# Row pairs in linear attention, and half-array products in longer blocks: one change to a two-layer hybrid trunk

## The chip, the cores and the metric

The kernel runs on one core of one Trainium2 chip. The metric is the device time of one execution in microseconds. Times are given for the kernel as a whole; the profile is one further execution, recorded by the hardware profiler.

## The reference: what is computed

The model is a trunk of two layers over 256 latent tokens and 256 context tokens of width 1024, all in fp32. In each layer one input projection feeds three token mixers and their gates. The mixers are latent attention with 8 heads (MLA), bidirectional gated linear attention with 4 heads (GLA) and neighbourhood attention with 8 heads. Their outputs are merged by gates, and a SwiGLU block follows. The change touches the two softmax mixers a little and the linear attention a lot. What the linear attention computes, cut to its core:

```python
q, k, v, log_a = ch(q), ch(k), ch(v), ch(log_a)      # chunks of 64 tokens
cum = jnp.cumsum(log_a, axis=3)
q_dec = q * jnp.exp(cum)
k_inv = k * jnp.exp(-cum)
k_end = k * jnp.exp(last - cum)
att = jnp.where(lower, einsum('bhncd,bhnsd->bhncs', q_dec, k_inv), 0.0)
o_intra = einsum('bhncs,bhnse->bhnce', att, v)
kv_chunk = einsum('bhncd,bhnce->bhnde', k_end, v)
# scan over chunks: state = decay * state + kv_chunk
o_inter = einsum('bhncd,bhnde->bhnce', q_dec, s_prev)
```

It is done forward and backward in time; context tokens come first and hand their final state to the latent tokens. In the last layer context tokens give no output, so only the two latent token tiles need attention there.

In the softmax mixers the latent queries see 512 keys (latent and context), the context queries 256 (context only); the latter are left out in the last layer.

## The kernel before, in words

Activations lie with features on the 128 partitions and the 512 tokens along the free dimension. The weight matrices are streamed from HBM in units of 128 x 1024 (`take`), each split by ScalarE (`hi`) and VectorE (`lo`) into two fp32r parts, and each product of the projections is three matmuls (`gemm`). The small products of the mixers are plain fp32; the profiler records each such product as two TensorE instructions.

The program isn't issued in the order in which it is written. `_Plan` records every operation with a price (`price`) and its dependencies, gives each a due time (TensorE's operations in the order recorded, the others backwards from who needs them), and `schedule` plays the engines against each other with those prices: each engine takes the ready operation with the earliest due time whose buffers have a free slot. There are 8 PSUM banks (`b`) and 70 SBUF slabs of 128 x 512 (`s`). The order that comes out is emitted as it is, and each engine then runs its own list in that order, waiting on semaphores. `drive` interleaves the recording: it runs the main work, a list of projections, and draws a filler generator along, so that the sum of the filler's yielded costs keeps pace with the mains' share done (`ftotal` is the sum at which the mains end). Lines 253 to 260 change the price of one kind of matmul: where the output has 64 partitions or fewer and the one before it went to another set of partitions, the second costs 56 ns (27 for 32 partitions).

The stages that matter here, in each layer:

- `fill1` (MLA) and `fill2` (neighbourhood attention) run `softmax_items` as filler: per head pair `hp`, key set `s` (0: latent queries, 1: context queries), query half `q` and head `e`, a score bank (`mas`, `nas`), the softmax, transposes into `PT` slabs (`mat`, `nat`), and `st_O`, which multiplies by the values. The two heads of a pair write to partitions 0-63 and 64-127 of one bank (`mao`, `nao`), so their products use different column halves of the array.
- `gla` is the filler of the next stage, whose mains are the values and gates of the linear attention (`zt`) and the merge of branch 1 (`z`, `proj`). `gla_prep` makes the cumulated decays: per head `hh` one bank `gc`, for each of four token tiles `t` a product with the upper triangle into partitions 0-63 and one with the lower into 64-127 (forward and backward). `ec` and `ei` are their exponentials, by which `qq` and `kk` are scaled.
- `kv(t)` transposes the scaled keys of one token tile (`gkt`, copied to `gkT`), and for each of its two chunks of 64 tokens multiplies keys by values: `gkv`, with 64 rows of the array (the chunk's tokens, partitions 0-63 or 64-127) and 128 columns, four heads into one bank. VectorE scales each head's block by the chunk's decay (`gkvs`).
- `att(t)` makes, for each direction `d`, the products of keys and queries of the four heads into one bank `gat`; the direction's 64 features are partitions 0-63 or 64-127, so again 64 rows and 128 columns. VectorE copies them under a mask (`attz`), and adds the two (`gatt`).
- `scan` carries the states (`gS`, on VectorE), and `o_tile` forms the output (`go`): values by `gatt`, queries by the states. Token tiles 2 and 3 (context) come first, then 0 and 1. After `gla`, its output `yB` is merged by branch 2, the last before the output projection (`wo`).

Of the kernel before, what the change touches and what calls it, by code (L numbers as in the profile page):

```python
# [9 lines left out]
F32 = mybir.dt.float32  # L10
# [171 lines left out]
class _Plan:  # L182
# [15 lines left out]
    def record(self, eng, name, args, kw):  # L198
        op = _Op()
        op.eng, op.name, op.args, op.kw, op.idx = eng, name, args, kw, len(self.ops)  # L200
        op.func = args[2] if name == "activation" else None
        w, r = [], []
        if "out" in kw:
            w.append(kw["out"])
            rest = list(args)
        else:
            w.append(args[0])
            rest = list(args[1:])
        for k, v in kw.items():
            if k == "accum_out":  # L210
                w.append(v)
            elif k != "out":
                rest.append(v)
        r = [v for v in rest if isinstance(v, _View)]
        w = [v for v in w if isinstance(v, _View)]
        if name == "copy_predicated" or (name == "matmul" and not kw.get("start", True)):
            r.append(w[0])
        deps = set()
        op.bufs = []
        op.allocs = []  # L220
        for v in r:
            g = v.region()
            deps.update(o for o, q in v.buf.writes if _meets(g, q))
        for v in w:
            g = v.region()
            if v.buf.space == "psum" and eng == "pe":
                prev = [o for o, q in v.buf.writes]
                deps.update(prev[-1:])
                deps.update(o for o, q in v.buf.reads)
            else:  # L230
                deps.update(o for o, q in v.buf.writes if _meets(g, q))
                deps.update(o for o, q in v.buf.reads if _meets(g, q))
        for v in r:
            v.buf.reads.append((op.idx, v.region()))
        for v in w:
            g = v.region()
            if v.buf.first is None:
                v.buf.first = op.idx
                op.allocs.append(v.buf)
            v.buf.writes = [x for x in v.buf.writes if not (g[4] is None and x[1][0] >= g[0] and x[1][1] <= g[1] and x[1][2] >= g[2] and x[1][3] <= g[3])]  # L240
            v.buf.reads = [x for x in v.buf.reads if not (g[4] is None and x[0] != op.idx and x[1][0] >= g[0] and x[1][1] <= g[1] and x[1][2] >= g[2] and x[1][3] <= g[3])]
            v.buf.writes.append((op.idx, g))
        for b in {id(v.buf): v.buf for v in r + w}.values():
            op.bufs.append(b)
            b.left += 1
        deps.discard(op.idx)
        op.deps = deps
        op.pin = self.last_pe if self.pinned else None
        op.cost, op.bytes = self.price(eng, name, w, r, kw)
        if eng == "pe":  # L250
            self.last_pe = op.idx
            rows = w[0].p1 - w[0].p0
            if name == "matmul" and r[0].dtype == F32 and rows <= 64:
                if self.lead and w[0].p0 not in self.lead:
                    op.cost = 56.0 if rows > 32 else 27.0
                    self.lead.add(w[0].p0)
                else:
                    self.lead = {w[0].p0}
            else:
                self.lead = set()  # L260
        self.ops.append(op)
        return op
# [227 lines left out]
def tile_trunk(ctx: ExitStack, tc: tile.TileContext, xin, wst, wm0, wmt, cbc_in, ct_in, cols_in, fin_in,  # L490
# [18 lines left out]
    if True:  # L509
# [215 lines left out]
        def softmax_items(lat_only, S_fn, V, heads, bias_fn, fin_fn, name):  # L725

            items = [(hp, s, q, e) for hp in range(heads // 2) for s in range(1 if lat_only else 2) for q in range(2) for e in range(2)]
            P, PT, PO = {}, {}, {}

            def st_S(it):  # L730
                hp, s, q, e = it
# [26 lines left out]
                    nc.scalar.copy(PT[hp, s, e][a][:, :, 128 * q : 128 * q + 128], ps[:, 2 * a : 2 * a + 2])  # L758
                return 107 * n

            def st_O(hp, s):
                n = 4 if s == 0 else 2
                if s == 0:
                    PO[hp] = bank(f"{name}o{hp}")
                pt = [PT.pop((hp, s, e)) for e in range(2)]
                for k in range(n):
                    for e in range(2):
                        c = 128 * hp + 64 * e
                        nc.tensor.matmul(PO[hp][64 * e : 64 * e + 64, 256 * s : 256 * s + 256], V[2 * s + k][:, c : c + 64], pt[e][k // 2][:, k % 2],
                                         start=(k == 0), stop=(k == n - 1))  # L770
                if s == 1 or lat_only:
                    w = 256 if lat_only else 512
                    fin_fn(hp, PO.pop(hp)[:, :w], w)
                return 429 * n

            n = len(items)
            pend = []
            for i in range(n + 4):
                if i < n:
                    yield st_S(items[i])  # L780
                if 2 <= i < n + 2:
                    it = items[i - 2]
                    yield st_T(it)
                    if it[2] == 1 and it[3] == 1:
                        pend.append((i + 1, it[0], it[1]))
                if pend and pend[0][0] <= i:
                    _, hp, s = pend.pop(0)
                    yield st_O(hp, s)
            for _, hp, s in pend:
                yield st_O(hp, s)  # L790


        NF = 5
# [134 lines left out]
        for l in range(L):  # L928
# [275 lines left out]

            def gla_prep(las):
                for hh in range(4):
                    ps = bank("gc", [128, 512])
                    for t in range(4):
                        for d in range(2):
                            nc.tensor.matmul(ps[64 * d : 64 * d + 64, 128 * t : 128 * t + 128],  # L1210
                                             las[t][:, 128 * hh + 64 * d : 128 * hh + 64 * d + 64], tri[d], start=True, stop=True)
                    ec, ei = slab("gec"), slab("gei")
                    nc.scalar.activation(ec, ps, AF.Exp, bias=zero)
                    nc.scalar.activation(ei, ps, AF.Exp, bias=zero, scale=-1.0)
                    ecv = ec.rearrange("p (c s) -> p c s", s=64)
                    nc.vector.tensor_copy(dec[0:64, hh], ecv[0:64, :, 63])
                    nc.vector.tensor_copy(dec[64:128, hh], ecv[64:128, :, 0])
                    nc.vector.tensor_tensor(out=kk[hh], in0=kk[hh], in1=ei, op=ALU.mult)
                    nc.vector.tensor_tensor(out=qq[hh][:, :NQ], in0=qq[hh][:, :NQ], in1=ec[:, :NQ], op=ALU.mult)
                    yield 1800  # L1220
# [80 lines left out]
            def gla():  # L1301
# [14 lines left out]
                    bufs.append(t)  # L1316
                ctx_out = not last

                def kv(t):
                    ps = bank("gkt", [128, 4, 128])  # L1320
                    for hh in range(4):
                        nc.tensor.transpose(ps[:, hh], kk[hh][:, 128 * t : 128 * t + 128], ident)
                    kt = slab("gkT")
                    nc.scalar.copy(kt, ps)
                    yield 430
                    for half in range(2):
                        r = slice(64 * half, 64 * half + 64)
                        c = 2 * t + half
                        pk = bank("gkv", [128, 4, 128])
                        for hh in range(4):  # L1330
                            nc.tensor.matmul(pk[:, hh], kt[r, 128 * hh : 128 * hh + 128], gv[t][r, 128 * hh : 128 * hh + 128], start=True, stop=True)
                        s = slab("gkvs", shape=[128, 4, 128])
                        for hh in range(4):
                            nc.vector.tensor_scalar(out=s[:, hh], in0=pk[:, hh], scalar1=dec[:, hh, c : c + 1], scalar2=None, op0=ALU.mult)
                        kvs[c] = s
                        yield 860

                def att(t):
                    w = slice(128 * t, 128 * t + 128)
                    a = slab("gatt")  # L1340
                    for d in range(2):
                        r = slice(64 * d, 64 * d + 64)
                        ps = bank("gat", [128, 4, 128])
                        for hh in range(4):
                            nc.tensor.matmul(ps[:, hh], kk[hh][r, w], qq[hh][r, w], start=True, stop=True)
                        nc.vector.copy_predicated(bufs[d], gmask[d], ps.rearrange("p a b -> p (a b)"))
                        yield 860
                    nc.vector.tensor_tensor(out=a, in0=bufs[0], in1=bufs[1], op=ALU.add)
                    atts[t] = a

                Sp = {}
                ys = {}
# [42 lines left out]
                for cf in ([4, 5, 6, 7], [0, 1, 2, 3]):  # L1395
                    tt = (cf[0] // 2, cf[0] // 2 + 1)
                    for t in tt:
                        yield from kv(t)
                        if t in ts:
                            yield from att(t)  # L1400
                    st = scan(cf, cf[::-1], Sp, st)
                    for t in tt:
                        if t in ts:
# [308 lines left out]
```

## Time and profile before

| | |
|---|---|
| median of 3 runs | 1548.5 us (1545.71, 1548.5, 1548.73) |
| profiled execution | 1543.93 us, span 1542.1 us |
| mean granted TensorE clock | 0.996 |
| TensorE busy | 1523.3 us (99%), 9566 matmul instructions |
| weight loads | 1311.6 us (85%) |
| VectorE (DVE) busy | 1089.3 us (71%), 2174 instructions |
| ScalarE (ACT) busy | 763.3 us (49%), 1363 instructions |
| `gkv`: 128 instructions, 372.8 to 1254.7 us | `gat`: 96, 379.6 to 1261.6 us |
| `gc`: 128 instructions, 345.9 to 1212.5 us | `mao`, `nao`: 160 each |

Layer 0 of the linear attention lies at about 334 to 482 us of the span, layer 1 at about 1184 to 1290. The duration that a row gives for one matmul is longer than the time it takes from the next one, since matmuls overlap in the pipeline; the chain of waits, which adds up without overlap, gives what a group really takes. Some matmul records can be missing from a trace.

### The profile page before, as it was taken

The numbers are of one execution on the slowest core, as the hardware profiler recorded it, in microseconds if no ns is written. First come the engines' busy times: TensorE is split into PE (matmuls) and PEld (weight loads), VectorE is DVE, ScalarE is ACT, GpSimd is POOL, SyncE is SP. The second block draws the span as 40 slices with busy tenths as digits, with TensorE's granted clock in tenths as the row PEclk, the third lists the DMA queues.
The fourth block names the chain that finished last, engine by engine and source line by source line (L and its number), as shares of the span: only waits on it lengthen the run. The fifth ranks groups of instructions, "written<-read, shape, count | busy, mean of one in ns | idle before, by whom it ended". The sixth has DMA issues, their size and how long they took to land.

```text
span 1542.1 us, 24547 instructions
## 1 busy us (share of the span) xinstructions
PE 1523.3 (99%) x9566; PEld 1311.6 (85%) x9566; DVE 1089.3 (71%) x2174; ACT 763.3 (49%) x1363; POOL 0.2 (0%) x4
## 2 busy tenths in 40 slices
PE   8999999999999999999999999999999999999998
PEld 4687787789877899888888889887998999999998
DVE  5799989989888789633333336898476797776565
ACT  4669745576223345332232234679567535564443
POOL 0000000000000000000000000000000000000000
PEclk9999999999999999999999999999999999999999
DMA  9442244533335775622223224432342234455553
GB/s 365 148 157 99 101 157 168 172 131 123 103 110 174 248 268 179 204 93 91 92 90 100 96 91 143 143 113 82 105 145 87 99 107 164 164 195 190 178 190 112
DMA packets 67157, 222.68 MB, mean 144 GB/s; under 512 B 7964, under 2 KB 8348, under 8 KB 67040
## 3 DMA queue, kind: packets, MB, share of 16 engines
q1 hardware_dynamic: 67040, 221.11, 42.1%
q8 instruction: 75, 1.23, 0.3%
q14 instruction: 42, 0.34, 0.1%
HBM read 220.03 MB, written 1.05 MB: 143 GB/s over the span
## 4 chain that ended last, share of the span: by engine, by line
PE 94%; ACT 3%; DVE 2%; issue 0%; DMA 0%; SPq 0%; DVEq 0%
PE z L486 22%; PE fg L486 12%; PE fu L486 12%; PE fo L486 12%; PE zt L486 8%; PE proj L486 7%; PE wo L486 4%; PE zf L486 2%; PE mas L486 1%; PE nao L486 1%; PE nas L486 1%; PE mat L486 1%; PE go L486 1%; PE nat L486 1%; PE mao L486 1%; PE gkv L486 1%
## 5 line engine op out<-in xcount | busy, mean ns | idle before, releaser
L486 ACT CAST hi<-raw 128x1024 fp32r<-128x1024 f32 (+3 forms) x305 | 313.5, 1028 | 507.4 <-PE z L486 115.4
L486 DVE TENSOR_TENSOR lo<-raw,hi 128x1024 fp32r<-128x1024 f32 (+3 forms) x305 | 364.5, 1196 | 170.3 <-ACT hi L486 167.2
L486 PE MATMUL z<-uh,hi 128*128 128x512 f32 (+2 forms) x632 | 227.2, 360 | 0.0
L486 PE MATMUL z<-uh,lo 128*128 128x512 f32 (+2 forms) x632 | 219.8, 348 | 0.7 <-DVE lo L486 0.7
L486 PE MATMUL z<-ul,hi 128*128 128x512 f32 (+2 forms) x632 | 220.3, 349 | 0.0
L486 DVE SCALAR_TENSOR_TENSOR junk<-wm,cbc 128x1024 bf16<-128x1024 f32 x132 | 160.7, 1217 | 7.8 <-DMA wm<-in_wmt 6.8
L486 PEld LDWEIGHTS z<-uh,hi 128*128 128x128 f32 (+1 forms) x632 | 118.3, 187 | 23.6 <-issue 7.5
L486 PEld LDWEIGHTS z<-uh,lo 128*128 128x128 f32 (+1 forms) x632 | 118.1, 187 | 18.1 <-DVE lo L486 0.9
L486 PEld LDWEIGHTS z<-ul,hi 128*128 128x128 f32 (+1 forms) x632 | 118.4, 187 | 15.8 <-issue 0.7
L486 PE MATMUL fo<-hh,lo 128*128 128x256 f32 (+1 forms) x408 | 127.5, 314 | 0.0
L486 PE MATMUL fo<-hl,hi 128*128 128x256 f32 (+1 forms) x408 | 127.4, 314 | 0.0
L486 PE MATMUL fo<-hh,hi 128*128 128x256 f32 (+1 forms) x408 | 127.2, 314 | 0.0
L486 PE MATMUL fg<-uf,lo 128*128 128x256 f32 (+1 forms) x344 | 115.1, 335 | 0.0
L486 PE MATMUL fg<-ug,hi 128*128 128x256 f32 (+1 forms) x344 | 114.8, 334 | 0.0
L486 PE MATMUL fg<-uf,hi 128*128 128x256 f32 (+1 forms) x344 | 114.8, 334 | 0.0
L486 PE MATMUL fu<-uf,lo 128*128 128x256 f32 (+1 forms) x336 | 113.6, 338 | 0.0
L486 PE MATMUL fu<-uf,hi 128*128 128x256 f32 (+1 forms) x336 | 113.6, 338 | 0.0
L486 PE MATMUL fu<-ug,hi 128*128 128x256 f32 (+1 forms) x336 | 113.4, 338 | 0.0
L486 PE MATMUL zt<-hi,uh 128*128 128x256 f32 x352 | 102.4, 291 | 0.0
L486 PE MATMUL zt<-hi,ul 128*128 128x256 f32 x352 | 99.5, 283 | 0.0
L486 PE MATMUL zt<-lo,uh 128*128 128x256 f32 x352 | 99.1, 282 | 0.0
L486 PEld LDWEIGHTS fo<-hh,lo 128*128 128x128 f32 x408 | 76.5, 188 | 5.4
(402 smaller groups left out, 3204.8 us busy)
## 6 DMA issues: line engine op xcount, KB each, us to landing
raw<-in_wst SPq DMA_DIRECT2D x257, 512.0 KB, 3.5
wm<-in_wmt SPq DMA_DIRECT2D x82, 512.0 KB, 3.9
raw<-in_wst SPq DMA_DIRECT2D x40, 448.0 KB, 3.2
wmr<-in_wm SPq DMA_DIRECT2D x9, 512.0 KB, 7.2
nab<-in_nab SPq DMA_DIRECT2D x16, 256.0 KB, 3.8
fr<-in_wst SPq DMA_DIRECT2D x10, 256.0 KB, 5.8
raw<-in_wst SPq DMA_DIRECT2D x6, 384.0 KB, 3.0
x<-in_xin SPq DMA_DIRECT2D x8, 256.0 KB, 5.1
```

Of the source, the lines that this page charges most:

```text
L486: getattr(eng[o.eng], o.name)(*[real(a) for a in o.args], **{k: real(v) for k, v in o.kw.items()})
```

## The change

Three groups of half-array products are put together, and one price of the planner follows.

- `st_O` is called once per head pair instead of once per key set: the products of both key sets follow one another, 12 per pair instead of 8 and then 4. The bank is taken at that point.
- `gla_prep` records the decay sums of two heads together, into two banks, ahead of either's exponentials.
- `kv` and `att` become `chunks`: after the transposes, the attention products of both directions, alternating between rows 0-63 and 64-127 of the array from product to product, then the state products of both chunks, alternating likewise, each row half into its own bank (four banks, two where the tile has no attention). The VectorE work follows: both masked copies, the scaling of both chunks, the sum. The costs yielded to `drive` change from 430 and 860 for each bank to 430 and 2400 (1200 without attention).
- The planner's price: a matmul with 64 rows or fewer now counts too, and two neighbours are a pair when they differ in row half or in column half.

```diff
-            if name == "matmul" and r[0].dtype == F32 and rows <= 64:
-                if self.lead and w[0].p0 not in self.lead:
+            deep = r[0].p1 - r[0].p0
+            if name == "matmul" and r[0].dtype == F32 and min(rows, deep) <= 64:
+                at = (r[0].p0, w[0].p0)
+                if self.lead and at not in self.lead:
                     op.cost = 56.0 if rows > 32 else 27.0
...
-            def st_O(hp, s):
-                n = 4 if s == 0 else 2
-                if s == 0:
-                    PO[hp] = bank(f"{name}o{hp}")
-                pt = [PT.pop((hp, s, e)) for e in range(2)]
...
+            def st_O(hp):
+                po = bank(f"{name}o{hp}")
+                for s in range(1 if lat_only else 2):
+                    n = 4 if s == 0 else 2
+                    pt = [PT.pop((hp, s, e)) for e in range(2)]
+                    for k in range(n):
+                        for e in range(2):
+                            c = 128 * hp + 64 * e
+                            nc.tensor.matmul(po[64 * e : 64 * e + 64, 256 * s : 256 * s + 256], V[2 * s + k][:, c : c + 64], pt[e][k // 2][:, k % 2],
+                                             start=(k == 0), stop=(k == n - 1))
+                w = 256 if lat_only else 512
+                fin_fn(hp, po[:, :w], w)
+                return 429 * (4 if lat_only else 6)
...
-                    if it[2] == 1 and it[3] == 1:
-                        pend.append((i + 1, it[0], it[1]))
+                    if it[2] == 1 and it[3] == 1 and (lat_only or it[1] == 1):
+                        pend.append((i + 1, it[0]))
...
                 for hh in range(4):
-                    ps = bank("gc", [128, 512])
-                    for t in range(4):
-                        for d in range(2):
-                            nc.tensor.matmul(ps[64 * d : 64 * d + 64, 128 * t : 128 * t + 128],
-                                             las[t][:, 128 * hh + 64 * d : 128 * hh + 64 * d + 64], tri[d], start=True, stop=True)
+                    if hh % 2 == 0:
+                        pc = [bank("gc", [128, 512]) for _ in range(2)]
+                        for j in range(2):
+                            for t in range(4):
+                                for d in range(2):
+                                    nc.tensor.matmul(pc[j][64 * d : 64 * d + 64, 128 * t : 128 * t + 128],
+                                                     las[t][:, 128 * (hh + j) + 64 * d : 128 * (hh + j) + 64 * d + 64], tri[d], start=True, stop=True)
+                    ps = pc[hh % 2]
...
-                def kv(t):
+                def chunks(t, att):
+
                     ps = bank("gkt", [128, 4, 128])
...
                     yield 430
+                    if att:
+                        w = slice(128 * t, 128 * t + 128)
+                        pa = [bank("gat", [128, 4, 128]) for _ in range(2)]
+                        for hh in range(4):
+                            for d in range(2):
+                                r = slice(64 * d, 64 * d + 64)
+                                nc.tensor.matmul(pa[d][:, hh], kk[hh][r, w], qq[hh][r, w], start=True, stop=True)
+                    pk = [bank("gkv", [128, 4, 128]) for _ in range(2)]
+                    for hh in range(4):
+                        for half in range(2):
+                            r = slice(64 * half, 64 * half + 64)
+                            nc.tensor.matmul(pk[half][:, hh], kt[r, 128 * hh : 128 * hh + 128], gv[t][r, 128 * hh : 128 * hh + 128], start=True, stop=True)
+                    if att:
+                        for d in range(2):
+                            nc.vector.copy_predicated(bufs[d], gmask[d], pa[d].rearrange("p a b -> p (a b)"))
                     for half in range(2):
...
+                    if att:
+                        a = slab("gatt")
+                        nc.vector.tensor_tensor(out=a, in0=bufs[0], in1=bufs[1], op=ALU.add)
+                        atts[t] = a
+                    yield 2400 if att else 1200
...
-                        yield from kv(t)
-                        if t in ts:
-                            yield from att(t)
+                        yield from chunks(t, t in ts)
```

More of the change, by code (lines that the diff above doesn't have):

```diff
@@ L252, in record @@
             rows = w[0].p1 - w[0].p0
-            if name == "matmul" and r[0].dtype == F32 and rows <= 64:
-                if self.lead and w[0].p0 not in self.lead:
+            deep = r[0].p1 - r[0].p0
+            if name == "matmul" and r[0].dtype == F32 and min(rows, deep) <= 64:
+                at = (r[0].p0, w[0].p0)
+                if self.lead and at not in self.lead:
                     op.cost = 56.0 if rows > 32 else 27.0
-                    self.lead.add(w[0].p0)
+                    self.lead.add(at)
                 else:
-                    self.lead = {w[0].p0}
+                    self.lead = {at}
             else:
@@ L727, in softmax_items @@
             items = [(hp, s, q, e) for hp in range(heads // 2) for s in range(1 if lat_only else 2) for q in range(2) for e in range(2)]
-            P, PT, PO = {}, {}, {}
+            P, PT = {}, {}
             def st_S(it):
@@ L759, in st_T @@
                 return 107 * n
-            def st_O(hp, s):
-                n = 4 if s == 0 else 2
-                if s == 0:
-                    PO[hp] = bank(f"{name}o{hp}")
-                pt = [PT.pop((hp, s, e)) for e in range(2)]
[L766 to L774, printed above, removed]
+            def st_O(hp):
[11 more added lines that the diff above has]
+                return 429 * (4 if lat_only else 6)
             n = len(items)
@@ L783, in softmax_items @@
                     yield st_T(it)
-                    if it[2] == 1 and it[3] == 1:
-                        pend.append((i + 1, it[0], it[1]))
+                    if it[2] == 1 and it[3] == 1 and (lat_only or it[1] == 1):
+                        pend.append((i + 1, it[0]))
                 if pend and pend[0][0] <= i:
[L787 to L790, printed above, removed]
+                    yield st_O(pend.pop(0)[1])
+            for _, hp in pend:
+                yield st_O(hp)
         NF = 5
@@ L1326, in kv @@
+                    for hh in range(4):
[5 more added lines that the diff above has]
+                            nc.vector.copy_predicated(bufs[d], gmask[d], pa[d].rearrange("p a b -> p (a b)"))
                     for half in range(2):
-                        r = slice(64 * half, 64 * half + 64)
@@ L1328, in kv @@
                         c = 2 * t + half
-                        pk = bank("gkv", [128, 4, 128])
-                        for hh in range(4):
-                            nc.tensor.matmul(pk[:, hh], kt[r, 128 * hh : 128 * hh + 128], gv[t][r, 128 * hh : 128 * hh + 128], start=True, stop=True)
                         s = slab("gkvs", shape=[128, 4, 128])
                         for hh in range(4):
-                            nc.vector.tensor_scalar(out=s[:, hh], in0=pk[:, hh], scalar1=dec[:, hh, c : c + 1], scalar2=None, op0=ALU.mult)
+                            nc.vector.tensor_scalar(out=s[:, hh], in0=pk[half][:, hh], scalar1=dec[:, hh, c : c + 1], scalar2=None, op0=ALU.mult)
@@ L1335, in kv @@
                         kvs[c] = s
[L1336 to L1349, printed above, removed]
+                    if att:
+                        a = slab("gatt")
+                        nc.vector.tensor_tensor(out=a, in0=bufs[0], in1=bufs[1], op=ALU.add)
+                        atts[t] = a
```

## The prediction, made before the changed kernel was run

> **What bounds the kernel now.** I read the page first, then the chain of waits over the linear-attention stages, then the rows of the tiles that change, then busy time by stretch.
>
> ```profile
> span 1542.1 us, 24547 instructions
> PE 1523.3 (99%) x9566; PEld 1311.6 (85%) x9566; DVE 1089.3 (71%) x2174; ACT 763.3 (49%) x1363; POOL 0.2 (0%) x4
> PEclk9999999999999999999999999999999999999999
> ```
>
> TensorE is busy 99% of the span at full granted clock, so the time is the sum of what TensorE issues, and a step pays only where it shortens that sum. DVE is busy 71% on average, but not evenly, which matters below. The profiled execution took 1543.93 us, 1.8 us of it outside the span; the median of the runs is 1548.5 us. I work out a difference from the trace and take it from the median, whose runs (1545.7 to 1548.7) lie above the profiled one.
>
> The next rows are the chain of waits in layer 0 (start us, length us, what, count). Each fp32 product appears as two TensorE instructions, here called passes, so `gkv x8` is one half's four heads.
>
> ```profile
> 217.63 14.33 PE zt L486 x120
> ...
> 345.93 0.37 PE gc L486 x4
> ...
> 358.64 1.02 PE gc L486 x16
> ...
> 364.82 1.02 PE gc L486 x16
> ...
> 371.00 0.44 PE gkt L486 x4
> 371.44 1.42 PE zt L486 x12
> 372.86 1.09 PE gkv L486 x8
> 373.95 2.31 PE zt L486 x18
> 376.26 1.08 PE gkv L486 x8
> 377.35 2.32 PE zt L486 x18
> 379.66 1.09 PE gat L486 x8
> 380.75 3.04 PE zt L486 x24
> 383.79 1.08 PE gat L486 x8
> ```
>
> Three prices come out of it. (1) A full-array `zt` pass costs 14.33/120 = 0.119 us. Behind a half-array block 18 of them take 2.31 us, not 18 x 0.119 = 2.15: each block costs 0.165 us after its end. (2) `gc`, whose passes alternate between the two column halves, takes 0.37 us for 4 passes and 1.02 for 16: 0.054 a pass and 0.155 once. So a half-array block carries 0.155 + 0.165 = 0.32 us whatever its length. (3) `gkv` and `gat`, whose passes all sit in one row half, take 1.085 for 8, or (1.085 - 0.155)/8 = 0.116 a pass: twice the price of a pass of `gc`, with the same 128 moving columns.
>
> **The change, part by part.** No instruction is added or removed on any engine or DMA queue; order, blocks and bank lifetimes change.
>
> *Chunk states with attention* (`chunks` for `kv` and `att`). For a token tile with attention there are now two `gkv` and two `gat` blocks of 8 passes: 4 x (1.085 + 0.165) = 5.00 us. Afterwards there is one block of 32 passes that alternate between row halves 0-63 and 64-127, each pair into two banks. If row halves pair as column halves do, it costs 0.32 + 32 x 0.058 = 2.18, a gain of 2.82; if they do not, 0.32 + 32 x 0.116 = 4.03, a gain of 0.97. Layer 0 has four such tiles and layer 1 two. Layer 1's two tiles without attention go from 2.50 to 0.32 + 16 x 0.058 = 1.25 (gain 1.25) or 2.18 (gain 0.32). Sum: 6 x 2.82 + 2 x 1.25 = 19.4 us paired, 6 x 0.97 + 2 x 0.32 = 6.5 unpaired.
>
> No row of this trace shows two row halves side by side, so 0.116 and 0.058 are the two bounds, with the slower rival's price beyond. The nearest rows are these (tiles' rows with min/median/max ns, then the timeline):
>
> ```profile
> L486 PEld LDWEIGHTS gkv<-tv,gkT x128: 182/188/188, 372.8 to 1254.7; 64*128 64x128 f32 x128
> L486 PE MATMUL gkv<-tv,gkT x128: 272/272/374, 372.8 to 1254.8; 64*128 64x128 f32 x128
> ...
> L486 PEld LDWEIGHTS gc<-const,gla x128: 132/137/137, 345.9 to 1212.4; 128*64 128x64 f32 x128
> L486 PE MATMUL gc<-const,gla x128: 272/273/323, 345.9 to 1212.5; 128*64 128x128 f32 x128
> ```
> ```profile
> 358.57 0.14 PEld L486 LDWEIGHTS gc<-const,gla 128*64 128x64 f32 x2
> ```
> ```profile
> 358.57 0.33 PE L486 MATMUL gc<-const,gla 128*64 128x128 f32 x2
> ```
>
> The last two rows are a window at the head of a `gc` block: two weight loads of 133 ns begin and end within 0.14 us, and two products of 323 ns within 0.33. So two column halves load and multiply side by side, start within 10 ns of each other. A load of 128 columns lasts 188 - 137 = 51 ns more than one of 64, or 0.8 ns a column, about 102 ns in all: if the two row halves had to load one after the other, 0.116 a pass would stay. I take the paired price, because the halves of the array are seen to work independently, loads included, in the one direction that the trace shows.
>
> The Trainium skill (TensorE: Matmul & The Clock Gate, "Part 3: Packing small matmuls — row/col tiling") says that products in different row groups start about 4 ns apart, and that a load overlaps a running product only where the row group differs. The second half does not hold here: with it, `gkv` passes in one row half would need load plus product, some 0.21 us, and the trace has 0.116. Its four row groups gave 3.07 times, not 4; at that efficiency (an estimate) a pass would be 0.076 and the 19.4 us some 16.
>
> What may break a block: its first `gkv` waits for the ScalarE copy `gkT` of the transposes. Between lie at least six main passes (0.71 us) and the 16 `gat` passes (0.9), which cover a copy of 0.6 us. The block takes four banks beside `gkt`'s one, of eight; the main products need two or three. I allow 0.5 us, for one or two broken blocks.
>
> *Decay sums of two heads* (`gla_prep`). The 64 passes of a layer stand in 7 blocks in layer 0 and 8 in layer 1; the first and last of layer 1:
>
> ```profile
> 1192.93 0.37 PE gc L486 x4
> ...
> 1211.74 1.02 PE gc L486 x16
> ```
>
> Heads 2 and 3 become one block (now two). The first blocks are short because the four `las` tiles come in one by one; with both heads recorded together each arrival serves two. That leaves 2 to 5 blocks a layer, so 5 to 11 switches go: 1.6 to 3.5 us, I take 2.2.
>
> *Values of both key sets* (`st_O`, layer 0 only).
>
> ```profile
> 160.83 1.88 PE mao L486 x16
> ...
> 174.77 1.01 PE mao L486 x8
> ```
>
> For each of four head pairs, in two attentions, blocks of 16 and 8 passes become one of 24: 8 x 0.32 = 2.6 us at most. The four transposed-probability slabs of the first key set now live until the second is done. In the `mao` stage DVE is at its limit (next rows), so I give the gain there nothing and keep 1.3 us for `nao`; bounds 0 and 2.6.
>
> *What a shorter TensorE runs into.* DVE's work does not shrink with it. Busy us of PE, PEld, DVE and ACT by stretch:
>
> ```profile
> 120.00:220.00 100.00, 96.11 (x211) 0.98 0.34 114
> ```
> ```profile
> 371.00:404.00 33.00, 33.00 (x236) 29.77 (x234) 30.96 (x83) 8.98 (x15) 0.00 (x0) 1.00 0.23 78
> ...
> 475.00:580.00 105.00, 105.00 (x557) 89.56 (x556) 81.77 (x125) 38.92 (x51) 0.00 (x0) 1.00 0.71 241
> ```
> ```profile
> 371.00:475.00 104.00, 104.00 (x606) 83.62 (x605) 91.45 (x248) 28.85 (x63) 0.00 (x0) 1.00 0.32 107
> 1218.00:1290.00 72.00, 72.00 (x573) 66.60 (x572) 64.20 (x172) 28.44 (x53) 0.00 (x0) 1.00 0.36 123
> ```
>
> (The first row is DVE alone.) The chunk stage of layer 0 holds 91.5 us of DVE work, and TensorE falls there from 104 to 104 - 4 x 2.82 = 92.7. Layer 1 holds 64.2, and TensorE falls from 72 to 72 - 8.1 = 63.9. TensorE has no idle time there today with DVE at 94% (371-404); the most that DVE reaches in a long stretch is 96%. At 96% layer 0 cannot go below 95.3 (2.6 lost) and layer 1 not below 66.9 (3.0 lost): 5.6 us. Some of it spills into 475-580, where DVE is at 78%; on the other side the fill now runs denser (its costs sum to 34080 of 42000 in layer 0, before 38240; 26480 of 28000 in layer 1, before 29600), and all of one tile's evictions queue on DVE at once, `gat` before `gkv`, so that the state scan starts later. I take 5 us of loss, bounds 0 and 10.
>
> The sum: -19.4 + 0.5 - 2.2 - 1.3 + 5 = -17.4 us, which gives 1548.5 - 17.4 = 1531 us.
>
> **The rivals.**
>
> *DVE does not bind.* The lost 5 us stay and `mao` gains its 1.3: -19.4 + 0.5 - 2.2 - 2.6 = -23.7, 1525 us. For it: the spill into 475-580. Against: 94 to 96% already.
>
> *The halves do not pair*, so the change does not do what it says: loads of the two row halves come one after the other, the pass stays at 0.116, and only switches are saved. -6.5 - 2.2 - 1.3 = -10, and DVE keeps its slack: 1538.5 us. For it: no row pair in the trace, and 0.116 is close to a load's 0.102. Against: the two loads in 0.14 us.
>
> *Evictions and slabs take the gain.* The Trainium skill (TensorEngine Tiling (Array Packing), "PSUM Bottleneck") warns that packing speeds the products and not the copies out of PSUM; that speaks against this change. As a mechanism here: DVE's evictions, in the order fixed by the plan, come late, each `go` waits for its scan, and the slabs held by `st_O` starve the `mao` stage, whose pool is small (70 slots; by the code 58 are held at its start: 16 input slabs, 32 of queries and keys, 4 values, 4 gates, `kr`, `lra`). That stage shows such a stop today:
>
> ```profile
> PEld mat L486 <- ACT map L486: 2.3, 1, 2.3
> ```
>
> One more of 2.3 us for each of the four head pairs and the full 10 us on DVE give -23.1 + 1.3 + 9.2 + 10 = about -3: 1546 us.
>
> *Slower: changing halves loses the early weight load.* Today the next load runs under the current product (0.116 a pass against 0.102 of load and about 0.11 of product). If a load for the other row half had to wait until the running product ends, each pass would cost both, 0.21. A block of 32 would take 0.32 + 6.7 = 7.0 (+2.0, six times), one of 16 would take 3.7 (+1.2, twice): +14.4 - 2.2 - 1.3 = +11, 1559 us. It turns slower above (6 x 4.68 + 2 x 2.18 + 3.5)/224 = 0.16 us a pass. Against it: `gc` changes halves at every pass and stays at 0.054.
>
> **How the numbers follow.** Forecast 1531 us (own range 1526 to 1536): 0.54. DVE does not bind, 1525: 0.16. No pairing, 1538.5: 0.16. Evictions and slabs, 1546: 0.07. Slower, 1559: 0.07. A measurement of this kernel tells 0.2%, 3.1 us, from no change. Faster than that are the first three and some of the fourth: 0.88. Within it: 0.05. Slower: 0.07. The range reaches to the second and past the third: 1519 to 1543, which leaves the last two out.
>
> **What would show it.** Pairing: a row of `gat` and `gkv` passes in one block of 32 that lasts about 2 us in the chain, so near 0.06 a pass; near 0.12 it did not pair, near 0.2 the slower rival holds. DVE: its share of the chunk stages above 96%, and waits of TensorE for `gS` or `gkvs` ahead of `go`, which are not there now. Merging: `mao x24` and `nao x24` in layer 0, and `gc x32`; several short rows in their place mean that blocks broke. Slabs: idle TensorE between 120 and 230 us above today's. I would be wrong at the root if TensorE's busy time fell by 17 us and the span did not.

## The result, and the profile after

| | before | after |
|---|---|---|
| median of the runs | 1547.9 us | 1527.65 us (1525.72 to 1528.92) |
| ratio | | 0.987 (95%: 0.9853 to 0.9887) |
| span of the profiled execution | 1542.1 us | 1525.7 us |

The changed kernel is 20.3 us faster; 17.4 was forecast. Its page:

```profile
span 1525.7 us, 24563 instructions
PE 1500.9 (98%) x9566; PEld 1298.0 (85%) x9566; DVE 1091.8 (72%) x2174; ACT 760.8 (50%) x1361; POOL 0.2 (0%) x4
```

The counts of matmuls and of VectorE's instructions are the same; TensorE's busy time fell by 22.4 us and the span by 16.4. The chain of waits in layer 0's chunk stage (start us, length us, what, count):

```profile
368.44 0.44 PE gkt L488 x4
368.88 1.42 PE zt L488 x12
370.30 1.09 PE gat L488 x16
371.39 0.89 PE gkv L488 x16
372.28 6.58 PE zt L488 x54
...
389.26 2.95 PE go L488 x24
```

The blocks stay whole, and 32 passes take 1.98 us where four blocks of 8 took 4 x 1.085. At the head of such a block, a window of 0.03 us shows two loads and two products begun together, as `gc` showed them before:

```profile
370.23 0.19 PEld L488 LDWEIGHTS gat<-gqk 64*128 64x128 f32 x2
```
```profile
370.23 0.38 PE L488 MATMUL gat<-gqk 64*128 64x128 f32 x2
```

The other merges came out too: `mao` and `nao` in blocks of 24 (one of `nao`'s four stands as 2 and 22), `gc` in 4 blocks a layer with one of 32 (before: 7 and 8).

```profile
196.28 2.74 PE mao L488 x24
```
```profile
259.14 2.74 PE nao L488 x24
...
344.45 0.59 PE gc L488 x8
347.23 1.02 PE gc L488 x16
348.57 0.59 PE gc L488 x8
356.43 1.90 PE gc L488 x32
```

Layer 1 looks different. Its chain runs through VectorE for 21 us (1225 to 1246), along the state scan; some of it, then TensorE's waits in 1200 to 1262 us (total us, times, longest):

```profile
1223.75 1.24 PE proj L488 x11
1224.98 0.03 issue
1225.02 1.23 DVE lo L488
...
1233.12 0.36 DVE gS L488
...
1244.87 1.15 DVE lo L488
1246.01 0.04 issue
1246.06 2.87 PE z L488 x22
```
```profile
PEld go L488 <- DVE gS L488: 4.4, 7, 1.6
...
PE go L488 <- DVE gS L488: 2.9, 5, 1.4
```

Where the time went, by stretches from the first product of one tile to the first of the next, in the two profiled executions:

| from - to | before | after | difference |
|---|---|---|---|
| `ku` - `nas`, layer 0 (holds `mao`) | 125.6 | 124.9 | -0.7 |
| `nas` - `gc`, layer 0 (holds `nao`) | 112.7 | 110.8 | -1.9 |
| `gc` - `gkt`, layer 0 | 25.0 | 23.9 | -1.1 |
| `gkt` - `wo`, layer 0 (chunks, scan, merge) | 186.6 | 174.7 | -11.8 |
| `wo` layer 0 - `mas` layer 1 | 479.7 | 479.3 | -0.4 |
| `mas` - `gz`, layer 1 | 146.9 | 148.4 | +1.5 |
| `gz` - `gkt`, layer 1 (holds `gc`) | 33.1 | 31.4 | -1.6 |
| `gkt` - `wo`, layer 1 (chunks, scan, merge) | 100.3 | 99.3 | -1.0 |
| `wo` layer 1 - last product | 218.7 | 218.1 | -0.6 |
| together | 1428.5 | 1410.8 | -17.6 |

Ahead of the first `ku` no product changes, yet that stretch took 107.6 us before, 108.7 after, and between 107.0 and 111.6 in the four profiles taken next. The medians carry this scatter of the start; the table does not, so the experiments are read with both. Medians of different rows below can also come from different chips; each ratio is to the kernel before, measured beside that run.

### The profile page after: what moved, and what is told of

Its sections match the earlier page's. It is cut to its first block, busy times and chain, and to the rows that moved or that the text cites. A ratio compares the mean times of both kernels' runs of the same rounds, so it can differ in the third digit from the quotient of the medians.

```text
span 1525.7 us, 24563 instructions
## 1 busy us (share of the span) xinstructions
PE 1500.9 (98%) x9566; PEld 1298.0 (85%) x9566; DVE 1091.8 (72%) x2174; ACT 760.8 (50%) x1361; POOL 0.2 (0%) x4
## 4 chain that ended last, share of the span: by engine, by line
PE 90%; DVE 5%; ACT 4%; issue 1%; DMA 0%; SPq 0%; DVEq 0%
PE z L488 20%; PE fo L488 12%; PE fu L488 12%; PE fg L488 12%; PE zt L488 8%; PE proj L488 6%; PE wo L488 4%; PE zf L488 2%; PE nao L488 1%; PE nas L488 1%; PE nat L488 1%; ACT k L488 1%; PE go L488 1%; PE qu L488 1%; PE mas L488 1%; PE mao L488 1%
## 5 line engine op out<-in xcount | busy, mean ns | idle before, releaser
L488 PEld LDWEIGHTS fo<-hl,hi 128*128 128x128 f32 x408 | 76.4, 188 | 5.5
```

The source lines that it names most:

```text
L488: getattr(eng[o.eng], o.name)(*[real(a) for a in o.args], **{k: real(v) for k, v in o.kw.items()})
```

## The experiments

All of them compute the whole output. "Sum" is the last line of the table above for that kernel's profile (before 1428.5, changed 1410.8), "layer 1" its stretch `gkt` - `wo` in layer 1, and "stops" what successive starts of TensorE exceed their usual step by in layer 1's linear attention. Some of these profiles have short stretches at half the granted clock, which the last section takes up; they are in the sums and in layer 1's column.

| kernel | median us | ratio to before (95%) | sum | layer 1 | stops |
|---|---|---|---|---|---|
| changed | 1527.65 | 0.987 (0.9853-0.9887) | 1410.8 | 99.3 | 5.5 |
| changed, again | 1528.36 | 0.9871 (0.9853-0.9889) | 1410.8 | 99.3 | 5.5 |
| no pairs | 1532.76 | 0.9903 (0.9875-0.9931) | 1413.5 | 99.5 | 2.6 |
| half by half | 1534.38 | 0.9919 (0.9906-0.9933) | 1415.5 | 99.6 | 1.3 |
| values apart | 1533.9 | 0.9912 (0.9889-0.9936) | 1416.5 | 100.9 | 5.5 |
| decays apart | 1532.18 | 0.9903 (0.9882-0.9924) | 1411.8 | 99.3 | 4.8 |
| chunks only | 1532.91 | 0.9924 (0.9909-0.9939) | 1414.6 | 99.3 | 5.5 |
| old price | 1531.82 | 0.9919 (0.9901-0.9936) | 1413.4 | 100.5 | 6.1 |
| half the scaling on ScalarE | 1525.03 | 0.9855 (0.9835-0.9876) | 1405.7 | 95.3 | 1.7 |
| all the scaling on ScalarE | 1520.84 | 0.9834 (0.9819-0.9849) | 1405.0 | 92.4 | 0.0 |
| the same, again | 1523.6 | 0.9847 (0.9832-0.9862) | 1405.1 | 92.4 | 0.0 |
| old pace | 1527.84 | 0.9878 (0.9865-0.9892) | 1409.0 | 98.2 | 3.0 |
| states first (the changed kernel's program) | 1528.55 | 0.9886 (0.9871-0.9901) | 1409.6 | 99.4 | 5.5 |

**No pairs.** In each block the halves follow one another instead of alternating.

```diff
-                        for hh in range(4):
-                            for d in range(2):
+                        for d in range(2):
+                            for hh in range(4):
...
-                    for hh in range(4):
-                        for half in range(2):
+                    for half in range(2):
+                        for hh in range(4):
```

> The changed kernel with the same blocks, but inside a block all gat and gkv products of one row half first, then those of the other, so that no two neighbours lie in different row halves. Theory (the gain of the chunk blocks is mostly the pairing): a pass goes from 0.0575 back to about 0.116 us, so TensorE issues 6 x 32 x 0.058 + 2 x 16 x 0.058 = 13.0 us more; layer 1 has up to 6.6 us of waits on gS that a slower TensorE would hide again. So the time rises by 6.5 to 13 us against the changed kernel, to 1534 to 1541 us, and gat plus gkv of a tile take about 3.9 us in the chain instead of 1.98. Rival (the gain is the fewer switches, and any order of products within a block is as good): no change, 1526 to 1530 us.

It is 5.1 us slower in the median and 2.7 in the sum: slower, so the order of products counts, but by less than the theory said. Layer 0's chunk stretch alone takes 3.3 us more (178.0 for 174.7); the sum is smaller because this profile took 1.7 less in `mas` - `gz`, where its clock stayed full. The chain shows why (this kernel, layer 0):

```profile
372.19 1.31 PE gat L488 x13
373.50 0.11 PE gkv L488
373.60 0.01 PE gat L488
373.61 0.11 PE gkv L488
373.71 0.00 PE gat L488
373.72 0.11 PE gkv L488
373.82 0.01 PE gat L488
373.83 1.11 PE gkv L488 x13
374.94 5.15 PE zt L488 x42
```

The block takes 2.75 us, not 3.9: `gkv` passes of rows 0-63 start between the last `gat` passes of rows 64-127. The halves overlap without being neighbours in the text, some passes deep.

**Half by half.** To size that, one change of half in a block instead of three.

```diff
+                    for d in range(2):
+                        r = slice(64 * d, 64 * d + 64)
+                        if att:
+                            for hh in range(4):
+                                nc.tensor.matmul(pa[d][:, hh], kk[hh][r, w], qq[hh][r, w], start=True, stop=True)
+                        for hh in range(4):
+                            nc.tensor.matmul(pk[d][:, hh], kt[r, 128 * hh : 128 * hh + 128], gv[t][r, 128 * hh : 128 * hh + 128], start=True, stop=True)
```

> The changed kernel with each chunk block ordered row half by row half: first gat and gkv of rows 0-63 (16 passes), then those of rows 64-127. The run without pairs, which changed halves three times in a block of 32, came out at 0.082 us a pass and not at 0.116. Theory (a row half runs its own short queue, and the products of the next half start about three passes before the last of this half are done, so that each change of half saves three passes of 0.112): with one change left a block of 32 spans 0.214 + 30 x 0.112 - 3 x 0.112 = 3.2 us from first to last start, 0.104 a pass, and the time in layer 0's chunk stage rises by 4 x 1.45 = 5.8 us against the changed kernel; the whole is 1532 to 1537 us. Rival (products of different halves overlap freely within the block, at any distance): 0.06 to 0.08 a pass and 1527 to 1531 us.

```profile
372.87 1.09 PE gat L488 x8
373.96 0.56 PE gkv L488 x5
374.51 0.11 PE gat L488
374.62 0.01 PE gkv L488
374.63 0.11 PE gat L488
374.73 0.01 PE gkv L488
374.74 0.11 PE gat L488
374.85 0.00 PE gkv L488
374.85 0.55 PE gat L488 x5
375.40 0.89 PE gkv L488 x8
```

From first to last start the block takes 31 steps of 0.104 us, as the theory said, 3.43 us in the chain. The last three `gkv` passes of the first half share their time with the first `gat` passes of the second. Two more changes of half (the kernel without pairs) bring 3.43 - 2.75 = 0.68, so 0.34 or three passes each; a change at every product brings 1.98. Layer 0's stretch `gkt` - `wo` rises from 174.7 to 180.7, 6.0 against the 5.8 worked out.

**Values apart**: `st_O` as before the change, the rest changed.

> The changed kernel with the values of the two key sets apart again, as before (two blocks per head pair in layer 0). Eight more switches at 0.32 us are 2.6 us if the merge was worth what its blocks cost. Theory (in the mao stage VectorE and the slabs held longer eat that gain, in nao it stays): 1.3 us longer than the changed kernel, about 1529 us. Rival A (the full price): 2.6 us longer, 1530 us. Rival B (the slabs held longer cost more than the switches): 1 us shorter or more, 1526.5 us or less, with less idle time of TensorE between 120 and 220 us.

The stretch with `mao` takes 124.9 us either way, the one with `nao` 112.7 against 110.8. So the merge gains nothing where VectorE is at its limit and 1.9 us in `nao` (5 blocks fewer), the shape of the theory. The size was missed: 6.3 us in the median and 5.7 in the sum, more than any of the three said. Most of the rest lies behind the edit: 0.6 in layer 0's decay sums, where a fifth block appears, 0.8 in its chunk stage, 1.6 in layer 1's. The last is no matter of order: TensorE's order in that stretch is the changed kernel's, product by product, and the 1.6 us arise in one stretch of 3.4 us at half the granted clock, behind the stops:

```profile
1244.90:1248.30 3.40, 2.13 (x13) 1.48 (x13) 3.33 (x7) 0.99 (x6) 0.00 (x0) 1.00 0.00 0
1248.30:1251.70 3.40, 3.40 (x18) 3.40 (x17) 3.37 (x14) 0.52 (x4) 0.00 (x0) 0.50 0.77 230
```

Why the first two rose was not isolated.

**Decays apart**: `gla_prep` as before the change, the rest changed.

> The changed kernel with the decay sums of each head apart again, as before. The changed kernel has 4 gc blocks a layer where the kernel before had 7 and 8. Theory (a block costs 0.32 us whatever its length): with 7 and 8 blocks again, 7 x 0.32 = 2.2 us longer than the changed kernel, about 1530 us. Rival (the later layers' waits on VectorE take it up, at least in layer 1, where TensorE waits for gS): 1 us longer or less.

The two stretches that hold `gc` grow by 1.1 us (7 blocks for 4) and 1.5 (8 for 4), 0.37 a block; layer 1's chunk stretch does not give it back (99.3 both times), so the rival falls. The median rose by 4.5, twice what was expected; in the profiles 2.8 of that lie ahead of the first `ku` (111.5 us against 108.7). The sum shows only 1.0, since this execution took 1.6 less in `mas` - `gz` of layer 1, which the last section explains.

**Chunks only**: both of these as before.

> Only the chunk blocks and the price are changed; the values of the two key sets and the decay sums stand apart as before. If the parts add up, the merged values are worth 8 x 0.32 and the merged decay sums 7 x 0.32 us together 4.8 us, and this kernel takes 1532 to 1533 us. If layer 1's waits on gS take up what the decay sums save there, it is 1 us less.

1532.91 us, as expected. But the medians do not add up: either step back alone cost 6.3 and 4.5 us, both together cost 5.3. What adds up is the stretches: 1.9 for `nao`, 1.1 and 1.6 for `gc`, as in the two runs apart. The chunk blocks and the price bring 13.9 of the sum's 17.6 us.

**Half, and then all, of the scaling on ScalarE.** The test of what layer 1 waits for:

```diff
                         for hh in range(4):
-                            nc.vector.tensor_scalar(out=s[:, hh], in0=pk[half][:, hh], scalar1=dec[:, hh, c : c + 1], scalar2=None, op0=ALU.mult)
+                            if half == 1:
+                                nc.scalar.activation(s[:, hh], pk[half][:, hh], AF.Copy, scale=dec[:, hh, c : c + 1])
+                            else:
+                                nc.vector.tensor_scalar(out=s[:, hh], in0=pk[half][:, hh], scalar1=dec[:, hh, c : c + 1], scalar2=None, op0=ALU.mult)
```

> The changed kernel with the decay scaling of every second chunk (half of gkvs) on ScalarE instead of VectorE: 16 operations a layer of 0.34 us, 5.5 us of VectorE's work a layer, go to an engine that is 40% busy there. Theory (in layer 1 VectorE's work in the scan stage sets the pace, so that TensorE waits for gS ahead of go): the 5.5 to 6.6 us that layer 1 loses come back for the most part: 3 to 6 us shorter than the changed kernel, 1522 to 1525 us, and TensorE's idle time between the first go of layer 1 and its last falls from about 5.5 us to under 2.5. Rival (the waits come from the order that the plan fixed, not from the amount of work): within 1.5 us of the changed kernel, with the waits on gS still there.

> The changed kernel with all of the decay scaling (gkvs) on ScalarE: 11 us of VectorE's work a layer instead of 5.5. With half of it moved TensorE's stops in layer 1 fell from 5.5 to 1.7 us. Theory (VectorE's load sets the pace of the scan): the rest of the stops goes too, 1 to 2 us less than with half, 1523 to 1525 us. Rival (ScalarE's copies and splits are delayed in turn): as with half or 1 to 2 us longer.

With half of it moved the stops fall to 1.7 us and the stretch to 95.3; with all of it they are gone and it takes 92.4, 7.9 less than before the change where 8.1 had been worked out for TensorE alone. The medians missed their ranges a little: with half of it 2.6 us less than the changed kernel where 3 to 6 stood, with all of it another 4.2 less where 1 to 2 stood. The start of the program is part of that (111.3, then 107.0 us ahead of the first `ku`). The plan is made anew for each of these kernels, so TensorE's order in layer 1 changes with the work that is moved. Busy us in layer 1's stage, the changed kernel and this one (PE, PEld, DVE, ACT):

```profile
1202.00:1270.00 68.00, 63.82 (x547) 58.26 (x546) 62.24 (x170) 27.43 (x52) 0.00 (x0) 1.00 0.38 122
```
```profile
1202.00:1270.00 68.00, 68.00 (x606) 64.32 (x605) 58.16 (x146) 39.70 (x89) 0.00 (x0) 1.00 0.44 140
```

VectorE's share falls from 92% to 86%, and TensorE issues 59 more matmuls in the same time, without a gap. The kernel beats both; beside the changed one on the same chip:

> The changed kernel once more, beside the next one on the same chip. Its ratio to the kernel before should be within 0.985 to 0.989, as first measured.

> The kernel with all of the decay scaling on ScalarE once more, on the same chip as the changed kernel. Theory (the 5.5 us of stops in layer 1 and three of its switches go): 5 to 7 us less than the changed kernel. Rival (the difference first seen was one of chips): within 2 us of it.

1523.6 us (1522.9 to 1524.55) against 1528.36 (1525.45 to 1529.32): 4.8 less, just under the 5 to 7 expected, and 5.7 in the sum.

**Old pace** (the yield of a chunk block 3440 and 1720 for 2400 and 1200), **states first** (the masked copies recorded behind the scaling) and **old price** (`rows <= 64` and the output's half alone) were meant to leave the amount of work as it is and to change its place in time.

> The changed kernel with the costs that the fill yields as before (430 + 3440 a tile with attention, 430 + 1720 without), so that the planner spreads the linear attention over more main work. Theory A (in layer 1 VectorE has too much work in too short a stretch): the waits on gS in layer 1 fall from 5.5 us to under 2 and the kernel takes 2 to 4 us less than the changed one, 1524 to 1526 us. Theory B (with the old costs the fill of layer 1 ends behind its mains, 29600 of 28000, and the last products come without cover): within 1.5 us of the changed kernel or longer.

> The changed kernel with the masked copies of the attention recorded behind the scaling of the states, so that the scan's inputs come 1.5 us earlier and the attention's later; the amount of work is the same. Theory (the amount of VectorE's work decides): within 1.5 us of the changed kernel, waits on gS in layer 1 still over 4 us. Rival (the order decides, since the state scan is the longer chain): 2 to 4 us less, and the waits on gS under 3 us.

> The changed kernel with the planner's old price: a product in the other row half costs the full 219 ns in the plan instead of 56, so the plan believes a chunk block to be 2.6 us longer than it is priced now. The products and their order in the text are those of the changed kernel. Theory (the price only shifts the plan's clock by a few us in a stage where TensorE always has main work): blocks stay whole, the time is within 1.5 us of the changed kernel, 1526 to 1529 us. Rival (the plan with the right price issues the scan's work too early, so that the waits on gS in layer 1 are the price's doing): 3 us less, with the waits on gS under 3 us.

The slower pace cuts the stops to 3.0 us, but the half-array products of `go` (queries by the states) fall into 14 blocks instead of 11, and 1.1 us is left of it in the stretch: theory A was too large, B right in size; its reason, last products without cover, was not looked at.

States first turned out to be no experiment. The planner goes by due times, and for this edit every engine's list comes out as in the changed kernel, instruction by instruction. So the run says nothing for its theory or its rival; it is the changed kernel a third time, 1528.55 us beside 1527.65 and 1528.36.

Neither theory held for the price: without it the kernel is 4.2 us slower in the median, 2.6 in the sum, with the chunk blocks whole. In layer 0's chunk stage (0.9) TensorE's order is unchanged, and one load waits 0.4 us for VectorE's `lo`. In layer 1's (1.2) the profile has 6.8 us at half clock, and behind it (0.8) 3.4 us more, so part of the sum is the clock's; how much the plan itself costs was not settled.

## Why the prediction was right, and where it was not

*The price of a pair held.* 0.32 + 32 x 0.058 = 2.18 us for a block was forecast; 1.98 in the chain and, as before the change, 0.165 behind it are 2.15. Layer 0's chunk stretch gained 11.8 where 4 x 2.82 = 11.3 stood.

*The unpaired bound was too dear.* 0.116 a pass holds inside one half, but a block of both halves overlaps at each change: 0.082 and 0.104 with three changes and one. The rival "the halves do not pair" is out by the trace; and even the order without pairs gains 5.00 - 2.75 - 0.165 = 2.1 us a tile, not the 0.97 that I gave it.

*Decay sums*: 2.2 forecast, 1.1 + 1.6 measured. *Values*: nothing in `mao` and 1.3 in `nao` forecast, nothing and 1.9 measured. Nothing in `mao` rests on "values apart": the 0.7 us of the table's first row were there only in the two profiles with the values apart and half the clock at about 127 to 135 us (the kernel before and "chunks only").

*The step that failed is the cap on VectorE.* "At 96% layer 0 cannot go below 95.3 (2.6 lost) and layer 1 not below 66.9 (3.0 lost)" gave 5.6 us, taken as 5; about 7 were lost, and all in layer 1: 8.1 worked out, 1.0 gained. Three more half-array blocks of `go` (11 for 8) are 1 us of it and stops 5.5. A busy share was the wrong measure. Layer 0 ran at a VectorE share as high, with no stop:

```profile
390.00:446.00 56.00, 56.00 (x333) 43.39 (x333) 52.74 (x154) 17.05 (x46) 0.00 (x0) 1.00 0.33 105
...
456.00:560.00 104.00, 104.00 (x521) 87.47 (x520) 84.98 (x130) 36.69 (x47) 0.00 (x0) 1.00 0.73 245
```

94% in its scan, and the stretch behind it, up from 78% to 82%, took the rest. In layer 1 TensorE stopped at 92%, waiting for the states of the scan. Moving VectorE's work away cured it, and spreading it did so in part. That the scan's chain against the place of `go` in the fixed order decided, and not the amount of work, is the likeliest reading, but it is not shown: no run moved `go` or the scan alone. The spill that I named as a reason against the loss did its work in layer 0, the late scan that I named as a reason for it in layer 1.

*That the total came out so near is partly luck.* By stretches 17.6 us were gained where 17.4 stood. The chunk blocks brought 12.8 (11.8 and 1.0) where 19.4 - 0.5 - 5 = 13.9 stood: layer 0 lost nothing to VectorE and no block broke, layer 1 lost more than twice its share. The decay sums and `nao` brought 1.1 more than forecast, the other stretches together 0.2. The 20.3 us of the medians hold the scatter of the start besides.

The rivals "slower" and "evictions and slabs" did not come about; in the stretch with `mao` the merged kernel is as fast as the one without the merge. (In the sum given for "evictions and slabs" the -23.1 does not come out of the terms, which give -19.4 + 0.5 - 2.2 - 1.3 = -22.4; its 1546 would be 1546.6.)

## What to carry to other kernels

Two products that each use half of the array's rows are worth putting side by side, each half into a bank of its own as here (one bank for both was not tried): a pass cost half, 0.058 us against 0.112, and a long block saved the price of switching, 0.32 to 0.37 us each. When the bound engine gets faster, look for the chain on the next engine that ends at a wait in the fixed order, and not only at that engine's busy share, which here did not tell the layer that stopped from the one that did not. Where a planner orders the program, see that an edit reaches the order before reading its time. And compare stretches between landmarks of the trace where the start of a program scatters by more than the effect.

## What the runs showed of the hardware

**Products start out of the order of the text.** In "half by half" all `gkv` of rows 0-63 stand before any `gat` of rows 64-127 in the program, and the rows above show three passes of them starting after its first. The Trainium skill (TensorE: Matmul & The Clock Gate, "Part 3: Packing small matmuls — row/col tiling") states that matmuls start and end strictly in program order; this trace does not agree where the two lie in different row halves.

**A stop may cost twice.** Early in layer 1's MLA TensorE stops: `mat` waits 2.1 us for VectorE's `map`. In the changed kernel's profile the granted clock fell to half behind it (the figure behind POOL's column); "old pace" has a stop at the same place and no fall; the kernel before had a fall in layer 0:

```profile
1031.70:1034.40 2.70, 2.70 (x9) 2.10 (x8) 2.49 (x6) 2.63 (x7) 0.00 (x0) 0.52 0.31 96
1028.00:1031.70 3.70, 1.61 (x10) 1.11 (x9) 2.58 (x6) 3.64 (x7) 0.00 (x0) 1.00 0.10 40
```
```profile
1029.00:1034.40 5.40, 3.35 (x18) 2.50 (x17) 4.25 (x10) 5.29 (x10) 0.00 (x0) 1.00 0.18 73
```
```profile
127.40:130.20 2.80, 2.80 (x10) 2.31 (x9) 2.59 (x7) 2.74 (x7) 0.00 (x0) 0.50 0.36 143
```

It is 1.5 us in layer 1's `mas` - `gz` (148.4 with it, 146.9 without), and the profiles have one or the other. Without it the changed kernel's sum would be 1409.3. Layer 1's linear attention has such stretches too, at its stops: 3.4 us in "no pairs", "values apart" and "decays apart", 6.8 in "old price", none in the other profiles. What one costs varies: 1.6 us in "values apart", where it came behind the stops, nothing to be seen in "decays apart" (99.3), where it came between them. The Trainium skill (the same page, "Part 1: The HAM clock gate") has the clock fall after an idle window of about 3.4 us; here it fell with TensorE busy 1.61 us of the 3.70 before, and in "values apart" with 2.13 of 3.40.
